# Projection columns in another order, and one head pair's keys and queries computed inside attention

## The chip, the cores and the metric

The kernel runs on one core of one Trainium2 chip. The metric is the device time of one execution in microseconds (us), the lower the better. Engines are named as in the profile: PE (TensorE, matmuls and transposes), DVE (VectorE), ACT (ScalarE), POOL (GpSimd), and SP, whose queue issues nearly all transfers from memory.

## The reference, cut to what matters

Two layers over 512 latent tokens and 256 context tokens of width 1024. Each layer has a token-mixing part with one input projection, whose output columns go to three groups of heads, and a SwiGLU part.

```python
IN_SIZES = (D_A, D_A, D_A, 2 * D_B, D_C, D_KV_C, D_KV_C)   # 384 384 384 512 384 128 128

def mixing_sublayer(h, hc, ...):
    qa, ka, va, zb, qc, kc, vc = split_cols(h @ w_in, IN_SIZES)
    qa_x, ka_x, va_x, zb_x, qc_x, kc_x, vc_x = split_cols(hc @ w_in, IN_SIZES)
    ...
    o_a = neighbourhood_attention(heads(qa, 6), heads(ka, 6), heads(va, 6), ka_x, va_x, rpb)
    o_b = spatial_gating(jax.nn.gelu(zb), w_s, b_s, g_sgu)
    ...
    o_c = gqa_latent(q_c, k_c, heads(vc, 2), kc_x, vc_x)
    y = merge_groups(o_a, o_b, o_c, g_out) @ w_o

for l in range(2):
    mod = split_cols((silu(c) @ w_mod[l] + b_mod[l]), 6 * (1024,))     # shifts, scales, gates
    h = modulate(x, sh1, sc1); hc = modulate(ctx, sh1x, sc1x)
    y, yc = mixing_sublayer(h, hc, ...)      # yc only in layer 0
    x = layer_norm(ALPHA * x + g1 * y) * ln1_g[l] + ln1_b[l]
    x = layer_norm(ALPHA * x + g2 * swiglu(modulate(x, sh2, sc2), ...)) * ln2_g[l] + ln2_b[l]
    # the context stream goes the same way in layer 0
```

The six heads of group A make three pairs; a pair's 128 columns of queries, keys or values fill one tile of 128 partitions.

## The kernel before, in words

**Products.** Every fp32 operand is split into a high part (fp32r) and the rest, and a product is three matmuls: high by high, high by low, low by high (`mm3`, lines 713 to 715). With 512 latent columns such a matmul is 128x512, with 256 context columns 128x256. `xh`, `xl` are the split latent tokens, `ch`, `cl_` the context tokens (`cb` in the profile).

**The weight stream.** `w_in` is cut into nine pieces of 256 columns, 1 MB each. Pieces 2, 3, 1 and 0 hold the gating, the queries and the keys of group C; 6 the keys of head pairs 0 and 1; 7 the keys of pair 2 and the queries of pair 2; 8 the queries of pairs 0 and 1; 5 the values of pairs 0 and 1; 4 the values of pair 2 and of group C. The class `Stream` loads each item of its list into one of two buffers `raw` (line 394, on SP's queue) and splits it into a weight slot `wa`, `wb` or `wc`: the high part in two halves on ACT (line 349), the low part of the first half on DVE and of the second on POOL (line 352). A buffer `raw` is free for the load after next when its reader is done. A slot is free when the piece's last matmul is done. Slots `wb` and `wc` are closed at the end of the projection, and the space of `wb` then holds the bias tables `tbz` of attention; `wa` stays. The list's order is `IN_ORDER`.

**Sums in the stream.** In layer 0 eight 1 MB items of `w_mod` stand in the same list, under the same two buffers. Each is not split but added up on DVE in four operations into `msum` (lines 658 and 661), four items to a modulation vector; the tail of a vector is a short product `mod_ps`, `rows`, `mod_tp`. `mi` says how many such items stand ahead of a piece. Layer 1 has none of these.

**Projection to columns.** `transposed` runs a piece: for each of its two halves, 24 matmuls on the context (`tc_ps`, where it is needed), 24 on the latent tokens (`tx_ps`), and then the half's evacuation. For keys and queries this is ACT to `kh` or `qh` (lines 1109 and 349) and DVE to `kl` or `ql` (line 1118, which reads what ACT has written); for values it is a copy to `vt`, transposes on PE (`vt_ps`, line 1133) and DVE copies to `va` or `vc` (line 1135). Each engine runs its instructions in the order in which the program was written, which a small model of times fixes while the kernel is built (`sd.tick`, `sd.spawn`).

**Attention.** After the projection a planner (`Plan`) takes a list of operations with engine, estimated time, dependencies, resources and a place, adds the offset of the operation's kind out of a table (`po`, one per layer), and writes them out in order. Scores (`scores_a`, line 1293) go to five banks `ring`; DVE adds the bias table and takes the minimum (line 1321); ACT takes the exponential (line 1333); PE turns the weights round (line 1341), multiplies by the values (line 1361). Two more banks, `aux`, serve the rest. Group C's queries and keys are turned in small steps `half` (line 1413). Table `wo` does the same as `po` for the output projection, `fo` for the feed-forward part.

Of the kernel before, what the change touches and what calls it, by code (L numbers as in the profile page):

```python
# [30 lines left out]
NH = 6  # L31
# [250 lines left out]
def tile_backbone(ctx: ExitStack, tc: tile.TileContext, io, out):  # L282
# [71 lines left out]
    class Stream:  # L354
# [27 lines left out]
        def pick(self, key):  # L382

            for slot in self.free:
                if slot == "a" or not (key[0] == "o" and self.in_phase):
                    return slot

# [134 lines left out]
    st = Stream()  # L522
    IN_ORDER = (2, 3, 1, 0, 6, 7, 8, 5, 4)

# [443 lines left out]
    for l in range(DEPTH):  # L968
# [46 lines left out]
        with ExitStack() as es:  # L1015
# [143 lines left out]
            if full:  # L1159
                sd.spawn(bias_windows())  # L1160
            transposed(6, (ev_qk(kh_, kl_, 0, 1.0), ev_qk(kh_, kl_, 1, 1.0)), (True, True))
            transposed(7, (ev_qk(kh_, kl_, 2, 1.0), ev_qk(qh, ql, 2, -0.125)), (True, full))
            transposed(8, (ev_qk(qh, ql, 0, -0.125), ev_qk(qh, ql, 1, -0.125)), (full, full))
            sd.spawn(scale_b(), 4.0)
            transposed(5, (ev_va(0), ev_va(1)), (True, True))
            transposed(4, (ev_va(2), ev_vc), (True, True))
            if full:
                st.finish_mods()
            sd.drain()

# [12 lines left out]
        def open_ring(width, n):  # L1183
# [19 lines left out]
            "bA": 5 if full else 6, "bC": 0, "pT a": 4, "p a": 4, "pT c": 0, "p c": 0, "aux": 2, "qn": 2, "mtmp": 2, "oT": 2, "ss": 5, "Q": 2,  # L1203
            "sC": 0, "win": 2, "raw": st.plan_raw(), "w": 1, **{f"tb{v}": 0 for v in range(6)},
        }, K["po"][l])
# [49 lines left out]
        for grp in ((2,), ())[l]:  # L1255
# [13 lines left out]
            mod_end.append(pn.op(DVE, 0.3, lambda md=md: (md.store(), aux.append(md.tp)), (prev,), 0.0, give=("aux",)))  # L1269
        assert st.free == ["a"]  # L1270
        o0_ops = st.plan_split(pn, n, first_c + 4.0, mod_end)
# [166 lines left out]
        for n, (kind, i) in enumerate(seq):  # L1438
# [4 lines left out]
            for d in range(2):  # L1443
                tk = ("aux",)
                if d == 0:
                    tk += (("sC",) if i else ()) if kind == "k" else ("Q",) if i < 2 else ("sC",)
                h = pn.op(PE, 0.17, call(half, n, d), (lo,) + tuple(pes_), p0 + 2.0, take=tk, kind="half")
# [14 lines left out]
        for un in units:  # L1462
# [5 lines left out]
            elif i % 2 == 0:  # L1468
                s_ = pn.op(PE, 0.05 + 0.165 * un.nch, call(scores_a, units[i:i + 2]), (), i - 1.4, take=(b, b), kind="scores " + un.kind)
            else:  # L1470
# [53 lines left out]
        def merge(key, src, cols, parts, perm, dst, deps, prio):  # L1524
# [12 lines left out]
            b_ = pn.op(ACT, 0.1 + (0.002 if perm else 0.0008) * n + 0.18 * (len(parts) - 1), call(gained, key, parts, perm), (a_,), prio, take=("mtmp",), give=("aux",), kind="gain")  # L1537
            c_ = pn.op(POOL, 0.1 + 0.0018 * n, high, (b_,), prio, kind="high")
            lo = pn.op(POOL, 0.1 + 0.0023 * n, low, (c_,), prio, give=("mtmp",), kind="low")
# [628 lines left out]
```

## Time and profile before

| | |
|---|---|
| time, median of 3 runs | 1659.42 us (1658.28 to 1660.36) |
| profiled execution, its own time | 1659.47 us |
| its span in the trace | 1657.7 us |
| mean granted TensorE clock | 0.994 |
| PE busy | 1614.0 us, 97% of the span |
| DVE / ACT / POOL busy | 1016.4 / 583.7 / 844.4 us |

The profiled execution lies in the middle of the runs, 0.05 us above their median, and 1.8 us of it lie outside the span. In the trace the projection of layer 0 to columns fills about 115 to 196 us, its attention 200 to 263 us; in layer 1 the projection ends at about 1118 us and attention runs to about 1225 us. A row of a list of instructions gives the start, the time, the engine, the line, the operation with what it writes and reads, and in brackets the idle time ahead of it with what ended it. A row of a table by stretches gives the stretch, its length, the busy time of PE, PE's weight loads, DVE, ACT and POOL, the granted clock, the share of the DMA engines and GB/s.

### The profile page before, as it was taken

Reading aid. Unit: us, or ns where it says so; the run is one execution under the profiler, and the core shown is the slowest. Engines: PE = TensorE matmul, PEld = TensorE weight load, DVE = VectorE, ACT = ScalarE, POOL = GpSimd, SP = SyncE. Lnnn points to the kernel's source line nnn. Section 1 sums busy time; section 2 is a strip of 40 time slices with the busy share of each in tenths; the row PEclk is TensorE's granted clock in tenths of the full one; section 3 lists DMA queues with packets and bytes.
Section 4 is the critical chain, followed back from the end, with each engine's and each line's share of the span. In section 5 each row is a group of like instructions: output and inputs, shape, how many; then the busy total and the mean of one; then the engine's idle time right before and its main releaser. Section 6 shows DMA issues by size and latency. Waiting matters only on the chain.

```text
span 1657.7 us, 26235 instructions
## 1 busy us (share of the span) xinstructions
PE 1614.0 (97%) x10546; PEld 1399.6 (84%) x10546; DVE 1016.4 (61%) x1645; ACT 583.7 (35%) x1008; POOL 844.4 (51%) x675
## 2 busy tenths in 40 slices
PE   7999999999999999999999999999999999999997
PEld 5998768899988888888888879887888988888886
DVE  7578657748578788777833297516757454334435
ACT  5422378737411111111111274217765422222211
POOL 1663443433346666655665346315334377666762
PEclk9999999999999999999999999999999999999999
DMA  9325480051244343443421223105124242322211
GB/s 358 99 89 190 147 303 29 2 204 52 81 155 159 109 145 115 134 140 107 148 96 51 77 87 93 49 1 166 39 80 150 75 142 102 102 97 83 101 51 51
DMA packets 47179, 184.81 MB, mean 111 GB/s; under 512 B 5248, under 2 KB 14848, under 8 KB 36048
## 3 DMA queue, kind: packets, MB, share of 16 engines
q1 hardware_dynamic: 45248, 179.11, 31.0%
q0 software_dynamic: 1664, 3.75, 0.9%
q8 instruction: 83, 1.36, 0.3%
q14 instruction: 40, 0.33, 0.1%
q10 hardware_dynamic: 144, 0.26, 0.0%
HBM read 178.87 MB, written 6.78 MB: 112 GB/s over the span
## 4 chain that ended last, share of the span: by engine, by line
PE 90%; DVE 3%; issue 2%; ACT 2%; POOL 1%; DMA 1%; DVEq 0%; SPq 0%; ACTq 0%; POOLq 0%
PE ff_ps L713 10%; PE ff_ps L715 10%; PE ff_ps L714 10%; PE y_ps L713 5%; PE y_ps L714 5%; PE y_ps L715 5%; PE aux L1361 4%; PE ring L1341 3%; PE ring L713 3%; PE ring L714 3%; PE ring L715 3%; PE ring L1309 2%; PE tx_ps L713 2%; PE tx_ps L714 2%; PE tx_ps L715 2%
## 5 line engine op out<-in xcount | busy, mean ns | idle before, releaser
L2017 POOL TENSOR_TENSOR x<-x,ytmp 128x1024 f32<-128x1024 f32 x90 | 248.4, 2785 | 28.3 <-DVE ytmp L2016 28.3
L352 POOL TENSOR_TENSOR gl<-sg,gh 128x512 fp32r<-128x512 f32 (+1 forms) x58 | 94.6, 1631 | 258.2 <-DVE gh L699 258.2
L661 DVE SCALAR_TENSOR_TENSOR msum<-raw,cs,msum 128x1024 f32<-128x1024 f32 x112 | 199.3, 1818 | 18.4 <-DMA raw<-in_w_mod_dram 18.4
L1992 DVE TENSOR_TENSOR sg<-sg,ff_ps 128x512 f32<-128x512 f32 (+1 forms) x58 | 34.4, 593 | 244.6 <-PE ff_ps L715 243.2
L2016 DVE TENSOR_TENSOR ytmp<-y_ps,g 128x512 f32<-128x512 f32 x180 | 118.6, 684 | 50.6 <-PE y_ps L715 50.4
L1991 ACT ACTIVATE sg<-ff_ps 128x512 f32<-128x512 f32 (+1 forms) x58 | 30.4, 523 | 274.4 <-PE ff_ps L715 274.4
L349 ACT ACTIVATE wc<-raw 128x1024 fp32r<-128x1024 f32 x52 | 52.8, 1052 | 149.9 <-PE y_ps L715 131.2
L349 ACT ACTIVATE wa<-raw 128x1024 fp32r<-128x1024 f32 x60 | 62.5, 1057 | 109.7 <-PE ff_ps L714 45.2
L352 POOL TENSOR_TENSOR wa<-raw,wa 128x1024 fp32r<-128x1024 f32 x29 | 75.5, 2604 | 46.1 <-ACT wa L349 46.1
L713 PE MATMUL y_ps<-wc,gh 128*128 128x512 f32 x248 | 98.2, 396 | 0.0
L714 PE MATMUL y_ps<-wc,gh 128*128 128x512 f32 x248 | 98.0, 395 | 0.0
L715 PE MATMUL y_ps<-wc,gl 128*128 128x512 f32 x248 | 97.9, 395 | 0.0
L352 POOL TENSOR_TENSOR wb<-raw,wb 128x1024 fp32r<-128x1024 f32 x25 | 65.7, 2627 | 60.3 <-ACT wb L349 60.3
L715 PE MATMUL ff_ps<-xh,wb 128*128 128x512 f32 x240 | 93.5, 390 | 0.0
L713 PE MATMUL ff_ps<-xh,wb 128*128 128x512 f32 x240 | 93.4, 389 | 0.0
L714 PE MATMUL ff_ps<-xl,wb 128*128 128x512 f32 x240 | 93.4, 389 | 0.0
L713 PE MATMUL ff_ps<-xh,wa 128*128 128x512 f32 x224 | 87.6, 391 | 0.0
L714 PE MATMUL ff_ps<-xl,wa 128*128 128x512 f32 x224 | 87.3, 390 | 0.0
L715 PE MATMUL ff_ps<-xh,wa 128*128 128x512 f32 x224 | 87.2, 389 | 0.0
L349 ACT ACTIVATE wb<-raw 128x1024 fp32r<-128x1024 f32 x54 | 55.1, 1055 | 86.8 <-DMA raw<-in_w_ffn_in_dram 46.6
L1341 PE MATMUL ring<-ident,p 128*128 128x128 f32 x528 | 76.3, 280 | 3.3 <-ACT p L1333 3.1
L352 POOL TENSOR_TENSOR wc<-raw,wc 128x1024 fp32r<-128x1024 f32 x24 | 63.9, 2663 | 21.8 <-ACT wc L349 21.8
(549 smaller groups left out, 5179.7 us busy)
## 6 DMA issues: line engine op xcount, KB each, us to landing
raw<-in_w_ffn_in_dram SPq DMA_DIRECT2D x44, 1024.0 KB, 4.9
raw<-in_w_mod_dram SPq DMA_DIRECT2D x40, 1024.0 KB, 5.4
raw<-in_w_ffn_out_dram SPq DMA_DIRECT2D x22, 1024.0 KB, 4.9
raw<-in_w_in_dram SPq DMA_DIRECT2D x18, 1024.0 KB, 4.8
wm<-in_w_mod_dram SPq DMA_DIRECT2D x8, 1024.0 KB, 11.7
raw<-in_w_o_dram SPq DMA_DIRECT2D x8, 1024.0 KB, 6.0
win<-t_dram SPq DMA_DIRECT2D x36, 128.0 KB, 2.8
tbz<-in_mask_dram SPq DMA_DIRECT2D x36, 128.0 KB, 3.2
```

What stands on the lines that cost most here:

```text
L349: nc.scalar.activation(out=o, in_=i, func=AF.Copy, scale=scale)
L352: e.tensor_tensor(out=o, in0=a, in1=b, op=ALU.subtract)
L661: nc.vector.scalar_tensor_tensor(out=o, in0=w[:, i, :], scalar=c, in1=o, op0=ALU.mult, op1=ALU.add)
L713: nc.tensor.matmul(o, lhsT=lh, rhs=rh, start=(i == 0), stop=False)
L714: nc.tensor.matmul(o, lhsT=lh, rhs=rl, start=False, stop=False)
L715: nc.tensor.matmul(o, lhsT=ll, rhs=rh, start=False, stop=(i == n - 1))
L1309: nc.tensor.matmul(un.S[:, s0:s0 + n], lhsT=q[:, t * P:(t + 1) * P], rhs=K[:, k0:k0 + n], start=(m == 0), stop=(m == 1))
L1341: nc.tensor.transpose(un.S[:, c:c + P], un.pt[:, j * P:(j + 1) * P], ident)
L1361: nc.tensor.matmul(u0.o[d * HD:(d + 1) * HD, 0:P], lhsT=un.vs[i], rhs=un.pT[:, i, :], start=(i == 0), stop=(i == u0.nch - 1))
L1992: nc.vector.tensor_tensor(out=sg, in0=sg, in1=ab[1], op=ALU.mult)
L2016: nc.vector.tensor_tensor(out=tmp[:, sl], in0=o, in1=G[1 if t >= NL else 0][:, sl], op=ALU.mult)
L2017: nc.gpsimd.tensor_tensor(out=x[:, t, :], in0=x[:, t, :], in1=tmp, op=ALU.add)
```

## The change

1. The pieces come in the order 2, 3, 1, 0, 5, 4, 6, 8, 7: values ahead of keys and queries, and piece 7 last. Of the eight `w_mod` items in layer 0, two stand ahead of piece 6 and six ahead of piece 8 (before: six ahead of piece 4 and two behind it; `mi` keys name the piece that they follow).
2. Piece 7 must be put into slot `wa`, piece 8 must not. Piece 7 is loaded and split in the projection, but its matmuls are operations of attention's planner (kind `late`): entries of six 128x512 or twelve 128x256 matmuls into an `aux` bank, then `late high` on ACT and `late low` on DVE. The scores of the third head pair wait for these; so do the steps `half` and the first split of the merged output.
3. The tables `po` and `wo` are replaced as a whole, every entry with another number; `fo` is the same. Of them the diff shows one line.

```diff
-K = dict(..., mi={5: 6, 4: 2}, my=9.0, ..., wo=({'add 0': -9.5, ...}, {...}), ..., po=({...}, {...}))
+K = dict(..., mi={4: 2, 6: 6}, my=9.0, ..., wo=({'add 0': 159.6, ...}, {...}), ..., po=({..., 'late': -40.3, ...}, {...}))
...
             for slot in self.free:
-                if slot == "a" or not (key[0] == "o" and self.in_phase):
-                    return slot
+                if slot != "a" and (key[0] == "o" and self.in_phase or key[0] == "in" and key[2] == 7):
+                    continue
+                if slot == "a" and key[0] == "in" and key[2] == 8:
+                    continue
+                return slot
...
-    IN_ORDER = (2, 3, 1, 0, 6, 7, 8, 5, 4)
+    IN_ORDER = (2, 3, 1, 0, 5, 4, 6, 8, 7)
...
-            transposed(6, (ev_qk(kh_, kl_, 0, 1.0), ev_qk(kh_, kl_, 1, 1.0)), (True, True))
-            transposed(7, (ev_qk(kh_, kl_, 2, 1.0), ev_qk(qh, ql, 2, -0.125)), (True, full))
-            transposed(8, (ev_qk(qh, ql, 0, -0.125), ev_qk(qh, ql, 1, -0.125)), (full, full))
-            sd.spawn(scale_b(), 4.0)
             transposed(5, (ev_va(0), ev_va(1)), (True, True))
             transposed(4, (ev_va(2), ev_vc), (True, True))
+            sd.spawn(scale_b(), 4.0)
+            transposed(6, (ev_qk(kh_, kl_, 0, 1.0), ev_qk(kh_, kl_, 1, 1.0)), (True, True))
+            transposed(8, (ev_qk(qh, ql, 0, -0.125), ev_qk(qh, ql, 1, -0.125)), (full, full))
             if full:
                 st.finish_mods()
+            w7 = ws(7)
             sd.drain()
...
-            "sC": 0, "win": 2, "raw": st.plan_raw(), "w": 1, ...
+            "sC": 0, "win": 2, "raw": st.plan_raw(), "w": 0, ...
...
+        late_qk, late_mm = [], []
+        for c, (hi, lo, sc, with_ctx) in enumerate(((kh_, kl_, 1.0, True), (qh, ql, -0.125, full))):
+            for d0, w_ in ((0, SEQ),) + (((SEQ, CTX),) if with_ctx else ()):
+                at, ops = {}, []
+                hh, hl = (ch, cl_) if d0 else (xh, xl)
+                for k0 in range(0, KC, 2 if w_ == SEQ else 4):
+                    ks = range(k0, k0 + (2 if w_ == SEQ else 4))
+                    def mm(...):
...
+                        for k in ks:
+                            wh, wl = (a[:, c * P:(c + 1) * P] for a in w7(k))
+                            for i, (a, b) in enumerate(((wh, hh), (wh, hl), (wl, hh))):
+                                nc.tensor.matmul(at["b"][:, 0:w_], lhsT=a, rhs=b[:, k, 0:w_], ...)
+                    ops.append(pn.op(PE, (0.227 if w_ == SEQ else 0.12) * 3 * len(ks), mm, ops[-1:], 2.0 + 0.1 * len(late_mm), take=("aux",) if k0 == 0 else (), kind="late"))
+                    late_mm.append(ops[-1])
...
+                a_ = pn.op(ACT, 1.1 if w_ == SEQ else 0.4, part_high, ops[-1:], 2.0, kind="late high")
+                late_qk.append(pn.op(DVE, 1.16 if w_ == SEQ else 0.42, part_low, (a_,), 2.0, give=("aux",), kind="late low"))
+        pn.op(None, 0.0, call(st.release, "in", l, 7), late_mm, give=("w",))
...
-                h = pn.op(PE, 0.17, call(half, n, d), (lo,) + tuple(pes_), ...
+                h = pn.op(PE, 0.17, call(half, n, d), (lo,) + tuple(pes_) + tuple(late_mm), ...
...
-                s_ = pn.op(PE, 0.05 + 0.165 * un.nch, call(scores_a, units[i:i + 2]), (), ...
+                s_ = pn.op(PE, 0.05 + 0.165 * un.nch, call(scores_a, units[i:i + 2]), late_qk if un.hd == NH - 2 else (), ...
...
-            c_ = pn.op(POOL, 0.1 + 0.0018 * n, high, (b_,), prio, kind="high")
+            c_ = pn.op(POOL, 0.1 + 0.0018 * n, high, [b_] + late_mm, prio, kind="high")
```

Lines of the kernel after stand three further down up to attention (DVE's 661 is 664, SP's 394 is 397) and 40 further down in it (the scores' 1293 is 1333).

The first place is the end of the sums in layer 0, on DVE. Before, this stands around the split of piece 4 (`raw_1856`), the piece that follows six items of `w_mod`; SP loads it into the buffer that `raw_1679` leaves:

```order
L661 SCALAR_TENSOR_TENSOR msum_1786<-raw_1679,cs_89,msum_1786 128x1024 x2
L1142 COPY vt_1828<-tc_ps_1749 128x256
L1135 COPY va_310<-vt_ps_1844 128x3x128
L661 SCALAR_TENSOR_TENSOR msum_1786<-raw_1731,cs_89,msum_1786 128x1024
L1135 COPY va_310<-vt_ps_1862 128x3x128
L661 SCALAR_TENSOR_TENSOR msum_1786<-raw_1731,cs_89,msum_1786 128x1024
L1135 COPY va_310<-vt_ps_1877 128x3x128
L661 SCALAR_TENSOR_TENSOR msum_1786<-raw_1731,cs_89,msum_1786 128x1024 x2
L352 TENSOR_TENSOR wa_71<-raw_1856,wa_71 128x1024
```

Now the piece that follows six items is piece 8 (also named `raw_1856` there); SP loads it into the buffer that `raw_1739` leaves. On DVE stands ahead of its split:

```order
L664 SCALAR_TENSOR_TENSOR msum_1678<-raw_1631,cs_89,msum_1678 128x1024 x2
L1121 SCALAR_TENSOR_TENSOR kl_832<-tx_ps_1725,kh_831 128x8x64
L1121 SCALAR_TENSOR_TENSOR kl_832<-tc_ps_1685,kh_831 128x256
L664 SCALAR_TENSOR_TENSOR msum_1678<-raw_1631,cs_89,msum_1678 128x1024 x2
L664 SCALAR_TENSOR_TENSOR msum_1678<-raw_1739,cs_89,msum_1678 128x1024 x3
L1121 SCALAR_TENSOR_TENSOR kl_832<-tx_ps_1807,kh_831 128x8x64
L1121 SCALAR_TENSOR_TENSOR kl_832<-tc_ps_1773,kh_831 128x256
L664 SCALAR_TENSOR_TENSOR msum_1678<-raw_1739,cs_89,msum_1678 128x1024
L664 SCALAR_TENSOR_TENSOR msum_1678<-raw_1811,cs_89,msum_1678 128x1024 x4
L352 TENSOR_TENSOR wb_110<-raw_1856,wb_110 128x1024
```

The last reading of `raw_1739` now stands behind the evacuation of `tx_ps_1807`, the second half of piece 6; before, the last reading of `raw_1679` stood ahead of all evacuations of the piece (5) that preceded the load's piece. On PE, piece 8's matmuls follow directly on those of `tx_ps_1807`, with no other work between.

The second place is SP's queue in the same stretch. Before, from the last piece but five on:

```order
L394 DMA raw_1731<-in_w_mod_dram 128x2x1024
L679 DMA g_dram_94<-rows_1779 4x512
L652 DMA bm_1787<-in_b_modh_dram 128x512
L394 DMA raw_1856<-in_w_in_dram 128x2048
L394 DMA raw_1920<-in_w_mod_dram 128x2x1024
```

and now:

```order
L397 DMA raw_1739<-in_w_mod_dram 128x2x1024
L397 DMA raw_1811<-in_w_mod_dram 128x2x1024
L397 DMA raw_1856<-in_w_in_dram 128x2048
L397 DMA raw_1862<-in_w_in_dram 128x2048
L1234 DMA win_2043<-t_dram_96 128x256
L1235 DMA tbz_2040<-in_mask_dram 128x256
```

Pieces 8 and 7 (`raw_1862`) are the last loads of the stretch, and attention's tables, whose space is slot `wb`, come behind them; before, two items of `w_mod` stood between the last piece and the tables.

The third place is the entry of attention in layer 1, on PE. Before, behind the last matmul of the last piece (values):

```order
L715 MATMUL tx_ps<-xh,wc 128x512
L1133 MATMUL vt_ps<-ident,vt 128x128 x6
L1509 MATMUL aux_10671<-ident,u 128x128 x4
L1293 MATMUL ring_10676<-kh,qh 128x256
L1293 MATMUL ring_10677<-kh,qh 128x256
```

and now, from the end of the second pair of score blocks on:

```order
L1333 MATMUL ring_10593<-kh,ql 128x256
L1333 MATMUL ring_10594<-kh,ql 128x256
L1290 MATMUL aux_10586<-xh,wa 128x512
L1290 MATMUL aux_10586<-xl,wa 128x512
L1290 MATMUL aux_10586<-xh,wa 128x512 x2
L1290 MATMUL aux_10586<-xl,wa 128x512
L1290 MATMUL aux_10586<-xh,wa 128x512
L1290 MATMUL aux_10587<-cb,wa 128x256 x12
L1381 MATMUL ring_10591<-ident,p 128x128 x4
```

No value transposes are left at the entry; two pairs of score blocks follow directly on the last matmul of piece 8, and late entries then stand before and between the first transposes of attention weights. In layer 0 the entry reads alike, with nearly the whole of the late work ahead of the first of these transposes.

More of the change, by code (lines that the diff above doesn't have):

```diff
@@ L1203, in tile_backbone @@
             "bA": 5 if full else 6, "bC": 0, "pT a": 4, "p a": 4, "pT c": 0, "p c": 0, "aux": 2, "qn": 2, "mtmp": 2, "oT": 2, "ss": 5, "Q": 2,
-            "sC": 0, "win": 2, "raw": st.plan_raw(), "w": 1, **{f"tb{v}": 0 for v in range(6)},
+            "sC": 0, "win": 2, "raw": st.plan_raw(), "w": 0, **{f"tb{v}": 0 for v in range(6)},
         }, K["po"][l])
@@ L1269, in tile_backbone, with mm, part_high, part_low @@
             mod_end.append(pn.op(DVE, 0.3, lambda md=md: (md.store(), aux.append(md.tp)), (prev,), 0.0, give=("aux",)))
-        assert st.free == ["a"]
+        assert st.free == []
+        late_qk, late_mm = [], []
[5 more added lines that the diff above has]
+                    ks = range(k0, k0 + (2 if w_ == SEQ else 4))
+                    def mm(c=c, w_=w_, at=at, hh=hh, hl=hl, ks=ks):
+                        if ks[0] == 0:
+                            at["b"] = aux.pop(0)
+                        for k in ks:
+                            wh, wl = (a[:, c * P:(c + 1) * P] for a in w7(k))
+                            for i, (a, b) in enumerate(((wh, hh), (wh, hl), (wl, hh))):
+                                nc.tensor.matmul(at["b"][:, 0:w_], lhsT=a, rhs=b[:, k, 0:w_], start=(k == 0 and i == 0), stop=(k == KC - 1 and i == 2))
+                    ops.append(pn.op(PE, (0.227 if w_ == SEQ else 0.12) * 3 * len(ks), mm, ops[-1:], 2.0 + 0.1 * len(late_mm), take=("aux",) if k0 == 0 else (), kind="late"))
+                    late_mm.append(ops[-1])
+                s_ = slice(d0, d0 + w_)
+                def part_high(hi=hi, sc=sc, at=at, s_=s_, d0=d0):
+                    if d0:
+                        copy_act(hi[:, 2, s_], at["b"][:, 0:CTX], sc)
+                    else:
+                        col_major(hi[:, 2, :], at["b"], sc)
+                def part_low(hi=hi, lo=lo, sc=sc, at=at, s_=s_, d0=d0, w_=w_):
+                    h, l_, src = hi[:, 2, s_], lo[:, 2, s_], at["b"][:, 0:w_]
+                    if not d0:
+                        h, l_ = (a.rearrange("p (c r) -> p r c", r=ROWS) for a in (h, l_))
+                        src = src.rearrange("p (r c) -> p r c", r=ROWS)
+                    nc.vector.scalar_tensor_tensor(out=l_, in0=src, scalar=sc, in1=h.bitcast(F32), op0=ALU.mult, op1=ALU.subtract)
+                    aux.append(at["b"])
+                a_ = pn.op(ACT, 1.1 if w_ == SEQ else 0.4, part_high, ops[-1:], 2.0, kind="late high")
+                late_qk.append(pn.op(DVE, 1.16 if w_ == SEQ else 0.42, part_low, (a_,), 2.0, give=("aux",), kind="late low"))
@@ L1446, in tile_backbone @@
                     tk += (("sC",) if i else ()) if kind == "k" else ("Q",) if i < 2 else ("sC",)
-                h = pn.op(PE, 0.17, call(half, n, d), (lo,) + tuple(pes_), p0 + 2.0, take=tk, kind="half")
+                h = pn.op(PE, 0.17, call(half, n, d), (lo,) + tuple(pes_) + tuple(late_mm), p0 + 2.0, take=tk, kind="half")
                 pes_.append(h)
@@ L1468, in tile_backbone @@
             elif i % 2 == 0:
-                s_ = pn.op(PE, 0.05 + 0.165 * un.nch, call(scores_a, units[i:i + 2]), (), i - 1.4, take=(b, b), kind="scores " + un.kind)
+                s_ = pn.op(PE, 0.05 + 0.165 * un.nch, call(scores_a, units[i:i + 2]), late_qk if un.hd == NH - 2 else (), i - 1.4, take=(b, b), kind="scores " + un.kind)
             else:
```

2 lines of the change are left out of this document (1 added, 1 removed).

## The prediction

> **What bounds the kernel now.** I read the page first: busy times, the granted clock, and the chain that ended last.
>
> ```profile
> span 1657.7 us, 26235 instructions
> PE 1614.0 (97%) x10546; PEld 1399.6 (84%) x10546; DVE 1016.4 (61%) x1645; ACT 583.7 (35%) x1008; POOL 844.4 (51%) x675
> PE 90%; DVE 3%; issue 2%; ACT 2%; POOL 1%; DMA 1%; DVEq 0%; SPq 0%; ACTq 0%; POOLq 0%
> raw<-in_w_in_dram SPq DMA_DIRECT2D x18, 1024.0 KB, 4.8
> ```
>
> PE is busy for 97% of the span and makes 90% of the chain. The change takes no matmul away, so it can only fill idle time of PE (43.7 us in the whole span) and slow stretches of its clock, or make new ones. The stretches that it touches are next: end of the projection and attention, of layer 0 (180 to 263) and of layer 1 (1118 to 1225).
>
> ```profile
> core 0: us, PE busy (x) PEld busy (x) DVE busy (x) ACT busy (x) POOL busy (x), PEclk, DMA share, GB/s
> 180.00:200.00 20.00, 18.25 (x108) 14.75 (x107) 15.25 (x18) 3.21 (x4) 6.03 (x8) 1.00 0.61 191
> 200.00:263.00 63.00, 61.41 (x667) 45.06 (x665) 37.55 (x132) 47.95 (x125) 22.32 (x26) 1.00 0.60 204
> 1118.00:1131.00 13.00, 9.76 (x87) 7.65 (x88) 5.81 (x17) 9.84 (x21) 6.07 (x9) 0.87 0.46 133
> 1131.00:1145.00 14.00, 12.77 (x137) 11.12 (x136) 9.19 (x31) 10.50 (x24) 9.15 (x12) 0.88 0.73 252
> 1145.00:1225.00 80.00, 77.44 (x809) 67.35 (x807) 59.30 (x143) 60.83 (x129) 28.45 (x38) 1.00 0.13 41
> ```
>
> Layer 0's attention has 1.6 us of idle PE to fill. Layer 1's entry has 3.2 + 1.2 us, and its clock is at 0.87 and 0.88: 0.13 x 13 and 0.12 x 14, 1.7 us each. Then the waits of PE, the first three rows from 42 to 200 us, the last from 1100 to 1145:
>
> ```profile
> PE tc_ps L715 <- POOL wa L352: 1.0, 1, 1.0
> PE mod_tp L684 <- DVE rows L677: 0.8, 1, 0.8
> PE vt_ps L1133 <- ACT vt L349: 0.7, 1, 0.7
> ...
> PE ring L1341 <- ACT p L1333: 2.5, 4, 1.7
> ```
>
> In layer 0 the projection hardly waits: once 1.0 us for a piece's split, and 0.7 and 0.8 us at attention's entry. In layer 1 the entry waits 2.5 us for the first attention weights.
>
> **Layer 0: the load of piece 8.** Before, the piece that follows six sums is piece 4. These rows show how early it came:
>
> ```profile
> 162.24 2.83 DVE L661 SCALAR_TENSOR_TENSOR msum<-raw,cs,msum 128x1024 f32<-128x1024 f32 x2
> 165.10 0.34 SPq L394 DMA_DIRECT2D raw<-in_w_in_dram  x1
> 169.87 2.01 ACT L349 ACTIVATE wa<-raw 128x1024 fp32r<-128x1024 f32 x2 [1.27 <-DMA raw<-in_w_in_dram]
> 175.21 0.39 PE L715 MATMUL tx_ps<-xh,wb 128*128 128x512 f32 x1
> 175.43 0.28 PE L713 MATMUL tc_ps<-cb,wa 128*128 128x256 f32 x1
> 176.56 2.36 POOL L352 TENSOR_TENSOR wa<-raw,wa 128x1024 fp32r<-128x1024 f32 x1
> ```
>
> The load is issued at 165.10, when the sum on its buffer has ended; PE ends the piece ahead of it at 175.43, 10.3 us later, and goes on at once. In the changed kernel piece 8 takes the buffer of `raw_1739`, and DVE's order puts the last operation on that buffer behind `kl` of piece 6's second half. That needs `kh` from ACT, and this needs the last matmul of piece 6. So the load can't be issued before PE has ended piece 6, and behind that matmul PE has nothing but piece 8. The steps from PE's end on, by the like steps before:
>
> ```profile
> 131.39 1.20 ACT L1109 ACTIVATE kh<-tx_ps 128x512 fp32r<-128x512 f32 x1 [5.09 <-PE tx_ps L715]
> 132.63 1.15 DVE L1118 SCALAR_TENSOR_TENSOR kl<-tx_ps,kh 128x512 fp32r<-128x512 f32 x1
> 133.67 0.41 DVE L1118 SCALAR_TENSOR_TENSOR kl<-tc_ps,kh 128x256 fp32r<-128x256 f32 x1
> 147.79 6.07 DVE L661 SCALAR_TENSOR_TENSOR msum<-raw,cs,msum 128x1024 f32<-128x1024 f32 x5
> 124.30 2.00 ACT L349 ACTIVATE wb<-raw 128x1024 fp32r<-128x1024 f32 x2
> 126.38 2.73 POOL L352 TENSOR_TENSOR wb<-raw,wb 128x1024 fp32r<-128x1024 f32 x1 [6.01 <-ACT wb L349]
> ```
>
> - ACT `kh` and both DVE `kl`: 131.39 to 134.08, 2.7 us.
> - one sum operation: 6.07 / 5 = 1.2 us; the load is issued 3.9 us after PE's end.
> - load until ACT starts: 169.87 - 165.10 = 4.8 us (as the page's median).
> - ACT's two halves 2.0 us, POOL's second half 2.7 us: 13.4 us in all.
> - on the first half of the weights PE can run ahead 12 matmuls of 128x256, which start 0.12 us apart (rows below): -1.4 us.
>
> That is 12.0 us of idle PE, against 1.0 us of waiting for POOL at the like place before: **+11.0 us**. The bounds: +12.4 if nothing runs ahead, and -1.0 if the load came in time, which the order excludes unless I misread the dependence. The six sums' other operations, `raw_1811` behind the load's release (4 x 1.2 = 4.8 us on DVE), run beside the load. Piece 7 is loaded after these and split while PE does piece 8's 96 matmuls, and stays hidden. What is late behind piece 8: the tables, now issued after its last matmul rather than under the last pieces; DVE's first table-added scores wait for them, and PE has the late entries for that time.
>
> **The clock after the idle.** No row before has an idle PE of 12 us; the nearest is 1118 to 1131, 3.2 us idle in 13, which cost 1.7 us of clock there and 1.7 us in the next stretch. I take 1.7 for the restart, bounds 0 and 3.4: **+1.7**. [...]
>
> **Layer 0: entry and filling.** The late work is half of a piece's shape twice over: 48 matmuls of 128x512 and 48 of 128x256. Their starts lie 0.22 to 0.23 and 0.12 us apart:
>
> ```profile
> 165.31 0.39 PE L714 MATMUL tx_ps<-xl,wb 128*128 128x512 f32 x1
> 165.53 0.39 PE L715 MATMUL tx_ps<-xh,wb 128*128 128x512 f32 x1
> 165.76 0.28 PE L713 MATMUL tc_ps<-cb,wb 128*128 128x256 f32 x1
> 165.87 0.28 PE L714 MATMUL tc_ps<-cb,wb 128*128 128x256 f32 x1
> ```
>
> 16.7 us of PE, moved and not added; its evacuation (two of ACT's `kh` kind, two pairs of DVE's) moves with it, and ACT, busy for 47.95 of 63 us, has room. At the entry the waits 0.7 (`vt`) and 0.8 (`mod_tp`, now inside piece 8) fall away. In their place the second pair of score blocks needs `ql` of piece 8's last half, 2.7 us after PE's end, and ahead of it stand 7 matmuls of 0.12: 1.9 us idle, and the late entries, which could fill it, are queued behind it on PE. Net **+0.4**. Filling in attention can win at most the 1.6 us of idle; I take **-1.0**, bounds -1.6 and +2 (two `aux` banks shared with the transposed outputs). Layer 0: 11.0 + 1.7 + 0.4 - 1.0 = +12.1.
>
> **Layer 1.** No sums stand in its stream, so piece 8 isn't held. Its entry before:
>
> ```profile
> 1118.80 0.88 PE L1133 MATMUL vt_ps<-ident,vt 128*128 128x128 f32 x6 [0.74 <-ACT vt L349]
> 1123.49 0.66 PE L1341 MATMUL ring<-ident,p 128*128 128x128 f32 x4 [0.27 <-ACT p L1333]
> 1126.83 0.98 PE L1341 MATMUL ring<-ident,p 128*128 128x128 f32 x4 [1.74 <-ACT p L1333]
> 1128.02 1.11 PE L1341 MATMUL ring<-ident,p 128*128 128x128 f32 x4 [0.21 <-ACT p L1333]
> 1118.12 0.31 POOL L1198 MEMSET tbz<- 128x256 f32 x1 [24.43 <-PE tx_ps L715]
> 1121.89 0.69 DVE L1321 CUSTOM_DVE_ANT_1 p<-ring,tbz 128x512 f32<-128x512 f32 x1 [1.22 <-POOL tbz L352]
> ```
>
> PE waits for weights whose tables start only with the end of the last piece. That chain stays, but 13.8 us of late work (48 x 0.227 + 24 x 0.12) now lie beside it. Filled: the 2.5 us of waits for `p` (-2.5), both slow stretches of the clock (-3.4, as gaps this small go), half of the 1.2 us idle in 1131 to 1145 (-0.6). Against it the wait for `ql`, 1.9 less the 0.4 of a context half that layer 1 doesn't have, in place of `vt`'s 0.74 (+0.8). **-5.7**; bounds -7.8 (all 4.4 of idle and 3.4 of clock) and -1 (the clock is lost all the same, as the transposes stay at the entry).
>
> **The tables `po` and `wo`.** Every place in attention and output projection may shift; the trace doesn't show by how much. The largest such effect I can price is what idle they govern: 1.6 and 2.6 us in the two attentions. I take 0, bounds -3 and +3.
>
> **Sum.** The trace's own execution took 1659.47: + 12.1 - 5.7 = 1665.87, and 0.05 less on the scale of the median, 1659.42: 1665.8.
>
> **Rivals.**
> - *The load of piece 8 isn't late* (ends faster). If the buffer is released earlier than I read, or the last sum needs no evacuation ahead of it, the +11.0 becomes -1.0 and the +1.7 goes: 1659.4 - 1.0 + 0.4 - 1.0 - 5.7 = 1652.1. The place is the gap on PE between pieces 6 and 8; the other terms make -6.3, so with stall and restart together below 3 us the time falls by more than 3.3. For it speaks that DVE came 10 us early before; against it the order of DVE, where the evacuation stands ahead of the last operation. Chance 0.12.
> - *The stall is there, but the rest gains as much*: filling and tables win their bounds (-1.6, -3) and layer 1 its -7.8, against 11.0 + 1.7 + 0.4: 1659.4 + 13.1 - 12.4 = 1660.1, within 0.2% (3.3 us, about what a measurement of this kernel can tell from no change). Chance 0.15.
> - *Layer 1 wins little, and the retuned tables lose*: the clock stays low among the transposes (-1), tables +3, restart +3.4: 1659.4 + 11.0 + 3.4 + 0.4 + 2 - 1 + 3 = 1678.2; half way there, from 1671 on, counts as this case. Chance 0.18.
> - *As forecast*, 1662.7 to 1671: 0.55.
>
> Slower therefore 0.73, same 0.15, faster 0.12. The likeliest case's own range is 1662.7 to 1671; with the same-case and the lower half of the rival above it the range is 1656 to 1675, which leaves out the faster case and the end of the dear one.
>
> **What the profile after would show.** Right: one wait of PE of 9 to 13 us in layer 0, at the first `tc_ps` on slot `wb`, put down to ACT's `wb` or the load, and piece 8's load issued some 4 us after the last `tx_ps` of piece 6; a slice of the clock below 9 just behind; in 1118 to 1145 a clock near 1.00 and no wait of PE for `p` over 1 us. Wrong: if that load is issued before piece 6 ends, the first rival holds. If the gap is there and the time is still no longer, layer 1 or the tables won more than I gave them, which the stretches 1118 to 1225 and those of the output projections would tell.

## The result, and the profile after

The changed kernel takes 1675.05 us (median of 4 runs, 1674.75 to 1676.36), the kernel before 1659.89 beside it: a ratio of 1.0097, 95% interval 1.0085 to 1.0109. It is 15.2 us slower; forecast were 6.4 us, with a range that ended at 1675, 0.05 us below the measured time. The sign and the main mechanism were right, the size was not.

The page of the changed kernel, the lines that answer to those of before (span, busy times, chain):

```profile
span 1673.3 us, 26248 instructions
PE 1617.1 (97%) x10546; PEld 1402.3 (84%) x10546; DVE 1012.8 (61%) x1645; ACT 584.5 (35%) x1008; POOL 847.8 (51%) x675
PE 86%; DVE 6%; issue 3%; ACT 3%; POOL 1%; DMA 1%; DVEq 0%; ACTq 0%; POOLq 0%
```

PE does the same 10546 matmuls; DVE's share of the chain has doubled. The starts of matching matmuls in the two traces say in which stage the time went:

| first or last matmul of a stage | before | after | difference |
|---|---|---|---|
| layer 0, last of group C's projection | 103.4 | 103.5 | +0.1 |
| layer 0, first of the feed-forward part | 444.4 | 463.2 | +18.8 |
| layer 0, first of its second product | 480.3 | 500.7 | +20.4 |
| layer 1, last of group C's projection | 1037.3 | 1057.9 | +20.6 |
| layer 1, first of the feed-forward part | 1339.5 | 1355.1 | +15.6 |

So layer 0 lost 20.4 us (forecast 12.1) and layer 1 won 4.8 (forecast 5.7). PE's waits in layer 0, first from 100 to 300 us, then from 340 to 500 us:

```profile
PE tc_ps L716 <- ACT wb L349: 9.8, 1, 9.8
PE ring L1333 <- DVE ql L1121: 2.0, 1, 2.0
...
PE tc_ps L718 <- DVE wb L352: 0.5, 1, 0.5
PE vt_ps L1136 <- DVE vt L1145: 0.4, 1, 0.4
...
PE ff_ps L718 <- DVE wb L352: 2.4, 1, 2.4
PE ring L1784 <- ACT n L1758: 1.8, 1, 1.8
PE ring L716 <- DVE cb L352: 1.6, 1, 1.6
PE ring L716 <- DVE cst L1748: 0.8, 1, 0.8
```

The wait of 9.8 us is the forecast one. The last three rows, 4.2 us in the output projection, were in no term of the sum; before, that stretch had only the wait `ff_ps <- DVE wb` and the full clock:

```profile
PE ff_ps L715 <- DVE wb L352: 2.3, 1, 2.3
430.00:437.00 7.00, 7.00 (x61) 7.00 (x60) 2.40 (x6) 2.29 (x4) 1.48 (x2) 1.00 0.77 279
```

How the longest of the three arises stands on ACT's list: the normalisation `n` is queued behind `htmp`, for which ACT waits 5.25 us for PE.

```profile
433.06 0.38 ACT L1956 ACTIVATE htmp<-ring 128x256 f32<-128x256 f32 x1 [5.25 <-PE ring L718]
433.34 1.14 ACT L1697 ACTIVATE n<-x,cst 128x1024 f32<-128x1024 f32 x1
```

Its scale then goes through POOL, and the last ACT step on `n` ends at 437.78, when PE goes on (437.84). The stall on piece 8 in its order, from the lists of ACT, DVE, SP and PE:

```profile
162.54 0.39 PE L718 MATMUL tx_ps<-xh,wa 128*128 128x512 f32 x1
162.97 1.10 ACT L1112 ACTIVATE kh<-tx_ps 128x512 fp32r<-128x512 f32 x1 [5.39 <-PE tx_ps L718]
165.09 0.42 DVE L1121 SCALAR_TENSOR_TENSOR kl<-tc_ps,kh 128x256 fp32r<-128x256 f32 x1
165.42 6.06 DVE L664 SCALAR_TENSOR_TENSOR msum<-raw,cs,msum 128x1024 f32<-128x1024 f32 x5
166.72 5.12 SPq L397 DMA_DIRECT2D raw<-in_w_in_dram  x2
171.65 2.00 ACT L349 ACTIVATE wb<-raw 128x1024 fp32r<-128x1024 f32 x2 [7.37 <-DMA raw<-in_w_in_dram]
172.75 0.58 PE L716 MATMUL tc_ps<-cb,wb 128*128 128x256 f32 x1 [9.82 <-ACT wb L349]
```

The load of piece 8 is issued at 166.72, 3.95 us after PE's last matmul of piece 6 (162.54 + 0.23; forecast 3.9), one sum operation into the five that begin at 165.42, and 4.9 us later ACT starts. The clock, by stretches (length, PE, weight loads, DVE, ACT, POOL, clock, DMA, GB/s): just behind the stall, in the output projection, at the first feed-forward block, and at layer 1's entry.

```profile
172.00:180.00 8.00, 6.78 (x30) 6.29 (x31) 1.23 (x1) 4.05 (x6) 5.21 (x5) 0.57 0.44 147
435.00:445.00 10.00, 7.51 (x48) 6.91 (x46) 0.99 (x2) 9.87 (x16) 4.84 (x6) 0.83 0.41 136
463.10:483.10 20.00, 17.60 (x118) 16.67 (x117) 12.75 (x14) 2.78 (x4) 7.68 (x5) 0.91 0.30 106
1125.30:1138.30 13.00, 11.70 (x83) 10.07 (x83) 4.75 (x11) 8.41 (x16) 6.42 (x9) 1.00 0.61 190
1138.30:1152.30 14.00, 14.00 (x128) 11.32 (x128) 6.56 (x20) 8.05 (x19) 3.76 (x6) 1.00 0.56 190
```

Layer 0's account: stall 9.8 + 0.5 less the 1.0 of before, +9.3; clock behind it 0.43 x 8, +3.4; entry 2.0 in place of 0.7 and 0.8, +0.5; output projection 4.2 of waits and 0.17 x 10 of clock, +5.9; clock at the feed-forward block 0.09 x 20, +1.8: 20.9, against 20.4 measured. Layer 1's entry is as forecast: clock 1.00 (3.4 us won), idle 1.3 us in place of 4.4 (3.1 won). Of these 6.5 us, 1.6 are lost again in layer 1's output projection, where the clock was 0.96 in the 40 us from 1260 (before 1.00 in the like stretch from 1245).

### The profile page after: what moved, and what is told of

Its sections match the earlier page's. It is cut to its first block, busy times and chain, and to the rows that moved or that the text cites. A ratio compares the mean times of both kernels' runs of the same rounds, so it can differ in the third digit from the quotient of the medians.

```text
span 1673.3 us, 26248 instructions
## 1 busy us (share of the span) xinstructions
PE 1617.1 (97%) x10546; PEld 1402.3 (84%) x10546; DVE 1012.8 (61%) x1645; ACT 584.5 (35%) x1008; POOL 847.8 (51%) x675
## 4 chain that ended last, share of the span: by engine, by line
PE 86%; DVE 6%; issue 3%; ACT 3%; POOL 1%; DMA 1%; DVEq 0%; ACTq 0%; POOLq 0%
PE ff_ps L716 10%; PE ff_ps L718 10%; PE ff_ps L717 10%; PE y_ps L716 5%; PE y_ps L717 5%; PE y_ps L718 5%; PE aux L1401 4%; PE ring L1381 3%; PE ring L716 3%; PE ring L717 3%; PE ring L718 3%; PE ring L1349 2%; PE aux L1290 2%; PE bank L718 2%; PE bank L716 2%
## 5 line engine op out<-in xcount | busy, mean ns | idle before, releaser
L352 POOL TENSOR_TENSOR wa<-raw,wa 128x1024 fp32r<-128x1024 f32 x30 | 79.0, 2634 | 45.7 <-ACT wa L349 45.6
```

Source lines behind the costliest of these rows:

```text
L352: e.tensor_tensor(out=o, in0=a, in1=b, op=ALU.subtract)
```

## The experiments

Two theories for the 20 us. The one of the prediction: the sums' place on DVE holds piece 8. The second, for the part that no term covered: the new numbers of `wo` make waits of their own. Rivals are named with each run.

**1. The six sums ahead of piece 4.**

```diff
-mi={4: 2, 6: 6}
+mi={5: 6, 4: 2}
```

> The changed kernel with the eight sums placed as six behind piece 5 and two behind piece 4, so that no sum stands between pieces 6 and 8. Theory (the last reading of the buffer behind the evacuation of piece 6 holds the load of piece 8): the wait of PE of 9.8 us on slot wb is gone, and with it the half clock of 172 to 180 us, which cost 0.5 x 4 + 0.35 x 4 = 3.4 us; 1675.0 - 9.8 - 0.5 - 3.4 = 1661.3, plus about 1 us for a split that still comes late: 1661 to 1663. Rival (DVE is full with sums and value evacuations at the same time, so the stall only moves to piece 4 or 6): a wait of 5 us or more stands elsewhere before 200 us, and the time stays above 1667.

1685.03 us, ratio 1.0153 (1.0138 to 1.0169): 10 us slower than the changed kernel. The rival was right. PE's waits from 100 to 210 us:

```profile
PE tc_ps L716 <- ACT wa L349: 13.6, 2, 10.5
PE mod_ps L676 <- DVE msum L664: 2.8, 1, 2.8
```

and the stretch with the first of them, where PE is busy for 7.02 of 18 us at a clock of 0.53:

```profile
130.00:148.00 18.00, 7.02 (x29) 4.48 (x26) 12.32 (x14) 2.00 (x2) 4.07 (x5) 0.53 0.61 196
```

Piece 4 now waits 10.5 us, and piece 6 another 3.2. DVE, busy for all 15 us from 115 to 130, does the sums late, and the load of piece 4 is issued only at 136.97. So the row that I read is not the whole cause: with the values first, the sums hold a later piece in this place too.

**2. The old `wo` in the changed kernel, and the new one in the kernel before.** The tables are exchanged, nothing else.

```diff
-wo=(<the changed kernel's numbers>)        # e2_old_wo, on the changed kernel
+wo=(<the numbers of before>)
-wo=(<the numbers of before>)               # e3_new_wo_in_before, on the kernel before
+wo=(<the changed kernel's numbers>)
```

> The changed kernel with the table wo of the kernel before, for both layers. Theory (the new numbers of wo are to blame for what layer 0's output projection lost): the waits of PE for cst, n and cb at 428 to 444 us, 4.5 us with the small ones, and the slow clock there and in the first feed-forward block (0.17 x 10 + 0.05 x 37.5 = 3.6 us) go: 1675.0 - 8.1 = 1667, if layer 1 doesn't change by more than 1. Rival (the waits come from attention's new order, whose ends feed the output projection): 1674 to 1676, with waits of 3 us or more still in that stretch.

> The kernel before with the changed kernel's table wo, nothing else. If the numbers by themselves make the waits: 1659.5 + 8 = 1667, with PE waiting for cst, n or cb in layer 0's output projection (about 410 to 445 us). If they only go with the new attention, or are as good as the old ones with the old one: within 2 us of 1659.5. If they suit no other order of attention than the one they were set with, it can be slower by more than 8.

With the old numbers 1669.85 us (1.0058, 1.0042 to 1.0075), 5.2 faster than the changed kernel; with the new ones in the kernel before 1665.66 (1.0037, 1.0025 to 1.0049), 6.2 slower. PE's waits from 400 to 480 us in the latter:

```profile
PE ff_ps L715 <- DVE wb L352: 2.4, 1, 2.4
PE ring L1744 <- ACT n L1718: 1.8, 1, 1.8
PE ring L713 <- DVE cb L352: 1.6, 1, 1.6
PE ring L713 <- ACT ring L1749: 1.0, 1, 1.0
PE ring L713 <- DVE cst L1708: 0.8, 1, 0.8
```

The same three waits, with the same lengths, under the old attention: the numbers make them, whatever precedes. In the former only the wait for `wb` is left there. The forecast 8.1 us came out as 5.2, in part since the slow clock of the feed-forward block (0.91, 1.8 us) stayed with the old numbers: it isn't the table's doing.

**3. PE kept busy in the gap.** Forty matmuls, read by nothing, between pieces 6 and 8:

```diff
+            if full:
+                dum = acc("dum")
+                for i in range(40):
+                    nc.tensor.matmul(dum, lhsT=xh[:, 0, 0:P], rhs=xh[:, 0, :], start=True, stop=True)
             transposed(8, ...)
```

> The changed kernel with 40 matmuls of 128x512 put into PE's queue between pieces 6 and 8, whose result is read by nothing: 9.1 us of work in the 10 us in which PE waits. It parts the wait from the clock. Theory (half rate after the gap comes from the idle): the granted clock stays at 1.00 from 165 to 180 us, where it was 0.50 to 0.65. At full rate PE catches up with POOL's half of the split, which ended 3.4 us after PE's start, so about 1.5 of the 3.4 us are lost again to that wait: 1673.0 to 1673.6, faster by 1.5 to 2. Rival (the clock there falls for another reason): the clock stays at 0.5 to 0.65 and the time within 0.5 of 1675.

1677.25 us (1675.18 to 1677.91), not faster. The clock through the gap and behind it:

```profile
165.00:172.00 7.00, 7.00 (x32) 5.79 (x32) 6.81 (x7) 1.38 (x2) 2.39 (x4) 1.00 0.50 167
172.00:176.00 4.00, 2.78 (x13) 1.84 (x11) 2.72 (x3) 1.93 (x3) 0.00 (x0) 1.00 0.63 197
176.00:180.00 4.00, 3.35 (x18) 3.06 (x19) 0.39 (x1) 1.47 (x5) 3.60 (x4) 0.69 0.58 240
```

It stayed at 1.00 until 176, where the changed kernel, idle for 9.8 us, had 0.50: so here the idle does set it. It fell then to 0.69, behind two waits of 0.9 and 0.8 us for the split's halves on ACT and DVE: part of the price came back later. This execution also waits 2.8 us for `vt` (DVE) near 116 us, where the changed kernel's has 0.4; the stage ahead of that wait (its last matmul is the first row of the table above) starts at 101.88 here and at 103.55 there, and the wait takes the 1.7 us back. So the run parts the clock from the idle in the trace, but gives no price for the clock alone: inconclusive in the time.

**4. The six sums behind piece 8**, and the same with the old `wo`:

```diff
-mi={4: 2, 6: 6}
+mi={4: 2, 8: 6}
```

> The changed kernel with the six sums behind piece 8 instead of ahead of it: piece 8 is loaded ahead of them, and piece 7, which attention needs only some 20 us after the end of piece 6, behind them. The stretch that moved the stall to piece 4 when the sums went ahead (DVE full with value evacuations) is left as it is. Theory (the stall of 9.8 + 0.5 us and the half rate behind it, 3.4 us, are the price of the place of the sums): no wait of PE over 3 us between 110 and 200 us, clock 1.00 there; 1675.0 - 13.7 = 1661.3, plus 1 us for the tail of the second sum (mod_ps, rows, mod_tp), which now stands at attention's entry: 1661 to 1664. Rival (DVE can't do six sums in this stretch at all, so that they stall whatever follows them): a wait of 5 us or more at the late entries or the scores, and 1668 or more.

> The same with the table wo of the kernel before as well: both causes undone. If they add up, what e2_old_wo won (5.2 us) comes off the time of e7_sums_behind_8: 1656 to 1659, the same as the kernel before or up to 0.2% faster, with layer 0 some 3 us slower than before and layer 1 some 5 faster. If they don't add up (the waits for cst, n and cb hide behind each other's shifts), above 1660.

1673.38 us (1.0087, 1.007 to 1.0104) and 1665.6 (1.0034, 1.0017 to 1.0051). The stall on piece 8 is gone, but the median is only 1.7 us lower, which the two intervals don't tell from nothing. PE's waits of the first of the two, 100 to 210 us:

```profile
PE vt_ps L1136 <- DVE vt L1152: 5.0, 1, 5.0
PE vt_ps L1136 <- DVE vt L1145: 2.6, 1, 2.6
PE mod_tp L687 <- DVE rows L680: 2.3, 1, 2.3
```

and from its list of DVE:

```profile
146.38 1.28 DVE L664 SCALAR_TENSOR_TENSOR msum<-raw,cs,msum 128x1024 f32<-128x1024 f32 x1 [7.83 <-DMA raw<-in_w_mod_dram]
...
152.92 0.41 DVE L1152 COPY vt<-tc_ps 128x256 f32<-128x256 f32 x1
```

DVE stands idle for 7.8 us until 146.38, waiting for a load of `w_mod`, and the copy `vt`, for which PE waits 5.0 us, is queued behind that sum. The old `wo` wins 7.8 us here and 5.2 there; the five runs with it spread from 1661.46 to 1669.12, so the two agree within the spread, and the two causes add up as far as that tells. The forecast of 1656 to 1659 missed by the new waits.

**5. The late entries ahead of the first scores**, on top of the last kernel:

```diff
-po=({..., 'late': -40.3, ...}, {..., 'late': 1.3, ...})
+po=({..., 'late': -400.0, ...}, {..., 'late': -400.0, ...})
```

> As e8_behind8_oldwo, with the offset of the kind late at -400 in both tables po, which puts five to nine late entries ahead of the first scores. Theory (the wait of PE for ql, 2.0 us in layer 0 and 1.3 in layer 1, is there because the late entries are queued behind the scores): both waits go, 3 us faster than e8_behind8_oldwo. Against it: in layer 0 piece 7 comes late now, and its matmuls may wait 1 to 3 us for its split; in layer 1 fewer late entries are left beside the wait for the first weights, which was 2.5 us before. Then no more than 1 us either way.

1672.38 us, 6.8 slower than without it. The wait for `ql` is gone in layer 1 (1.3 us); in layer 0 the kernel that this one builds on had none any more, so that half of the theory had nothing to win. Other waits came: from 180 to 290 us

```profile
PE mod_ps L611 <- DMA raw<-in_w_mod_dram: 2.8, 2, 2.0
```

and in layer 1 waits for `p` and `oa` of 4.0 us in all, against 1.9 without the edit. From the table's starts, layer 1's part is 4.2 us longer in this profile and layer 0's 0.3; 1.6 us were lost ahead of both, where nothing was changed. The theory fell: in layer 1 the late entries are worth more beside the first weights than ahead of the first scores.

**6. Three of four sum operations left out**, of the changed kernel and of the kernel before:

```diff
             for i in range(2):
                 for s in range(2):
+                    if self.l == 0 and self.kind in (2, 3) and self.k and i + s:
+                        continue
```

> The changed kernel with three of the four operations of each of layer 0's sums left out, except in the first item of each vector (so the vectors are wrong; all eight loads stay). It takes the sums' time off DVE without moving an item in the list. Theory (the stall ahead of piece 8 is sums that DVE couldn't finish in time between the evacuations): the load of piece 8 is issued before piece 6 ends, no wait of PE over 3 us between 110 and 200 us, and 1675.0 - 13.7 = 1661.3, 1660 to 1663. Rival (values ahead of keys stall PE by their own evacuations on DVE, sums or not): waits for vt or va of 3 us or more, 1667 or more.

> The same left out of the kernel before, as the control. In it PE waits for no sum, so at most the 1.0 us for POOL's split of piece 4 and the 0.8 us at attention's entry can go: 1658 to 1660. If it falls by more than 3 us, the sums cost time in the old order too, by a way that the waits don't show, and the difference of e10_nosum_after has to be read against it.

1666.27 us (1.0041, 1.0026 to 1.0056) and 1662.85 (1.0024, 1.0015 to 1.0034). In the first SP issues the load of piece 8 long before PE ends piece 6 (at 166.25), and PE doesn't stop:

```profile
148.88 2.96 SPq L397 DMA_DIRECT2D raw<-in_w_in_dram  x2
...
166.02 0.39 PE L720 MATMUL tx_ps<-xh,wa 128*128 128x512 f32 x1
166.25 0.28 PE L718 MATMUL tc_ps<-cb,wb 128*128 128x256 f32 x1
```

That is the stall's cause, taken away at its source: 8.8 us. Of the forecast 13.7, most of the rest is in two places: a wait of 3.2 us for `vt` at 126 us, and a clock of 0.91 from 180 to 200 us (1.8 us). The wait doesn't come from the values' own evacuations, as the rival has it. The copy `vt` stands on DVE behind the one sum operation that is left of its item, and this waits for its load:

```profile
128.30 1.28 DVE L666 SCALAR_TENSOR_TENSOR msum<-raw,cs,msum 128x1024 f32<-128x1024 f32 x1 [4.46 <-DMA raw<-in_w_mod_dram]
129.51 0.41 DVE L1147 COPY vt<-tc_ps 128x256 f32<-128x256 f32 x1
```

The control missed: leaving the operations out also moves the vector's tail ahead in the written order; PE waits 2.9 us for `msum` there, and the clock is 0.77 in the 15 us from 148. It can't be used to correct the first number.

**7. The late entries without the values ahead**, in layer 0 (the slot rule is set to match: there piece 4, not 8, must not take `wa`):

```diff
-    IN_ORDER = (2, 3, 1, 0, 5, 4, 6, 8, 7)
+    IN_ORDER = ((2, 3, 1, 0, 6, 8, 5, 4, 7), (2, 3, 1, 0, 5, 4, 6, 8, 7))
...
-mi={4: 2, 6: 6}, wo=(<the changed kernel's numbers>)
+mi={5: 6, 4: 2}, wo=(<the numbers of before>)
```

> Layer 0 with the late entries but without the values ahead: pieces in the order 2, 3, 1, 0, 6, 8, 5, 4, 7, sums where they were before (six behind piece 5, two behind piece 4), piece 7 in attention; layer 1 as in the changed kernel; old table wo, new po. It parts the order of the pieces from the late entries. Theory (layer 0 lost by the order, not by the late entries): no wait of PE over 3 us in 110 to 200 us, layer 0 within 2 us of before, layer 1 5.5 us faster: 1652 to 1656. Rival (the late entries cost in layer 0, where attention had only 1.6 us of idle to fill): 1657 to 1661, with waits in 200 to 280 us.

1652.38 us (1652.1 to 1653.62), ratio 0.9959 (0.9944 to 0.9974): the lowest median of all, and faster than the kernel before. PE's largest waits from 100 to 290 us:

```profile
PE aux L1419 <- DVE oT L1414: 1.0, 1, 1.0
PE mod_tp L687 <- DVE rows L680: 0.8, 1, 0.8
```

Layer 0's first feed-forward matmul starts 2.1 us earlier than before and layer 1's 7.0 earlier; 1.6 us of both were there already at the end of group C's projection, ahead of the change. So in layer 0 the late entries, and the new `po` with them, cost nothing and won nothing that can be told (0.4 us); the order of the pieces, with the sums' place that goes with it, and the table did. That the order has no place for the sums that costs nothing isn't shown: three were tried.

**8. The change in layer 1 alone**, with the new and the old `wo` in layer 1 (layer 0's lists, order and tables as before):

```diff
+    IN_ORDER = ((2, 3, 1, 0, 6, 7, 8, 5, 4), (2, 3, 1, 0, 5, 4, 6, 8, 7))
...
+        for c, (hi, lo, sc, with_ctx) in enumerate(() if full else ((kh_, ...), (qh, ...))):
```

> The change in layer 1 alone: order of the pieces, late entries and both tables as in the changed kernel in layer 1, and as in the kernel before in layer 0. Theory (the two layers' effects are apart): layer 0 ends when it did before, and layer 1 keeps the 4.8 us that it won: 1659.5 - 4.8 = 1654.7, 1653.5 to 1656. Rival (layer 1 started 20 us later in the changed kernel and its gain hangs on that, by weights that were loaded earlier): 1657 or more.

> e6_l1_only (1653.4 us) with the table wo of the kernel before in layer 1 too. In e2_old_wo the stretch of layer 1 was 0.7 us shorter with the old numbers: 1652 to 1653.5. If layer 1's new numbers are as good or better: 1653.5 to 1655.

1653.4 us (0.9963, 0.9952 to 0.9975) and 1654.49 (0.997, 0.9959 to 0.9981): layer 1's gain stands by itself, and its `wo` numbers can't be told apart. Their intervals overlap with that of run 7, so the late entries in layer 0 have no gain of their own to show.

## Why the prediction was right or wrong, point by point

- **The load of piece 8** (+11.0): right. Issue 3.95 us after PE's end against 3.9, 9.8 + 0.5 us of idle against 12.0, so +9.3; POOL's half cost nothing: POOL ended it at 176.18, and PE, whose 128x256 matmuls start 0.21 us apart there at a clock of 0.50 (0.12 elsewhere), came to the second half of the weights at 176.32. Run 6 shows that the sums hold it, runs 1 and 4 that another place for them only moves the stall.
- **The clock** (+1.7, bounds 0 to 3.4): the right cause (run 3) at the upper bound, 3.4 us. The 1.7 was my estimate from a stretch with 3.2 us of idle; no run shows it behind a gap of this length, and after 9.8 us of idle the clock was 0.57 for 8 us. That stall and clock together came to 12.7 us, as forecast, is in part luck: two misses of 1.7 us cancel, though the slow clock is also what hid POOL's half (an estimate: with 0.12 us from one start to the next in place of 0.21, PE would have come to that half about 1 us ahead of POOL's end).
- **Entry and filling of layer 0** (+0.4 and -1.0): measured +0.5 for the entry and, as the rest of the account, about -0.5.
- **Layer 1** (-5.7): -4.8. The steps named won more (6.5 us at the entry, with a wait for `ql` of 1.3 against 1.5), and the output projection, in which no loss was forecast, gave 1.6 back.
- **The tables** (0, bounds -3 to +3): this step failed. I bounded them by the idle time that attention had before, which bounds what new numbers can win, not what they can lose. The output projection had no idle to read a bound from, and it lost 5.9 us. The runs of experiment 2 show the table `wo` as the cause, in both directions: put into the kernel before it costs 6.2 us, taken out of the changed kernel it gives 5.2 back. `po` has no part in it that shows: run 7 has the new one. Which of `wo`'s numbers does it isn't shown.
- **A term that was missing**: 1.8 us of slow clock at the first feed-forward block of layer 0. It isn't the table's: it stays with the old `wo` in the changed kernel, and it is absent with the new `wo` in run 1 and in the kernel before. The last section shows where the wait ahead of it lay in two traces.
- **The sum** with what was measured: 9.3 + 3.4 + 0.5 - 0.5 + 5.9 + 1.8 - 4.8 = 15.6 us, the difference of the two spans (1673.3 and 1657.7), against 6.4 forecast.
- **The rivals**: the dear one (1671 and more, 0.18) came true, but with the tables over their end, the restart at its end, and layer 1's clock restored at the entry, not lost.

## What to carry to other kernels

Read for each load which instruction frees its buffer, and what stands ahead of that instruction on its engine: an evacuation that waits for PE there turns a prefetch into a stall of the whole load and split (here 9.8 us of PE). A set of schedule offsets that is replaced wholesale can lose far more than the idle that stands in its stage before (here 5.9 us in layer 0's output projection, which had none to read); exchange it alone, in both kernels, before judging the change that came with it. And take a change apart by layer and by part: with the late entries in both layers but the old order in layer 0 and the old `wo`, the kernel was 7 us faster than before instead of 15 slower, and the change in layer 1 alone was worth 5 to 7.

## What was not expected of the hardware

After 9.8 us without work the granted clock stood at 0.50 from 172 to 176 us and 0.65 from 176 to 180: some 6 us at half the clock from PE's first matmul on (172.75 to 178.80). The forecast had 1.7 us lost to it; here it was 3.4 (0.43 x 8), with one more wait of 0.5 us inside.

A wait of 2.3 to 2.7 us at the same place (the first feed-forward block of layer 0, `ff_ps <- DVE wb`) stands in ten of the kernels: before, after, those of runs 1 to 5, and the first of run 8. Six of these ten profiles show a clock of 0.91 in the 20 us around it (1.8 us lost: the changed kernel, the old `wo` in it, runs 3, 4 and 5) and four 1.00 (the kernel before, the new `wo` in it, run 1, and the change in layer 1 alone), with nearly the same busy time of PE (17.25 to 17.67 us). What decides between them isn't shown; the traces of the kernel after and the kernel before show where the wait lay against the moments at which the granted clock changes. In each of these two traces such moments lie whole multiples of 3.41 us apart; in the changed kernel they are, among others, 165.15, 178.80, 438.22, 441.63, 472.35 and 475.76, in the kernel before 1127.03, 1130.44, 1140.68 and 1144.09. Here are stretches of 3.41 us, counted from such moments, around the wait, for the changed kernel and then for the kernel before (PE's busy time is the first number behind the length, the clock the third from the end):

```profile
468.94:472.35 3.41, 1.01 (x9) 0.81 (x8) 3.38 (x5) 0.00 (x0) 0.00 (x0) 1.00 0.18 31
472.35:475.76 3.41, 3.41 (x19) 3.41 (x18) 0.03 (x1) 0.00 (x0) 0.73 (x1) 0.50 0.97 344
```

```profile
447.77:451.18 3.41, 2.77 (x24) 2.57 (x22) 3.41 (x2) 0.14 (x1) 1.64 (x1) 1.00 0.00 0
451.18:454.60 3.42, 1.72 (x14) 1.73 (x15) 2.27 (x4) 0.00 (x0) 0.74 (x1) 1.00 0.47 129
454.60:458.01 3.41, 3.41 (x30) 3.41 (x30) 0.00 (x0) 0.38 (x1) 0.00 (x0) 1.00 1.00 375
```

In the first the whole wait lies in one stretch (2.40 us without work), and the next stretch runs at 0.50. In the second it lies across two (0.64 and 1.70 us), and the clock stays at 1.00. No limit follows: elsewhere in the changed kernel's trace a stretch with 1.03 us of idle (1291.55 to 1294.96) was followed by a clock of 0.50. The six slow profiles are also those of the six kernels, of the ten, whose `mi` isn't that of before; whether their earlier slow stretches set where the wait falls wasn't tested.

The 6 us at half the clock, in the same stretches: PE came back inside the one from 171.98 to 175.39, which had 1.24 us of idle and a clock of 0.50; the next one, to 178.80, had no idle and 0.50 as well, and behind it the clock was 1.00.
